# Three dense products tied ahead of the first steps of the band stage and of the latent stage

## The chip, the cores and the metric

The kernel runs on one core of one Trainium2 chip. The metric is the device time of one execution in microseconds (us). The time before is 3204.06 us, the median of three runs (3197.32 to 3205.81).

## The reference, cut to what matters

Two layers of a hybrid streaming encoder are run over 1152 tokens: 1024 of one prompt and 8 x 16 of running streams, model width 1024. Each layer makes one combined input projection, three kinds of attention out of its columns, an output projection and an MLP:

```python
z = h @ w_in                    # h = rmsnorm(x); columns of all three head groups
q_lat, ckv, kr, gq, gk, gv, g_lr, g_out, cq, ck, cv = split(z)
o_mla = latent attention        # q = rmsnorm(q_lat) @ w_qup, keys and values out of ckv, block-causal, 6 heads
o_gla = gated linear attention  # recurrence over chunks of 64, 4 heads
o_ca  = band attention          # each chunk of 64 sees itself and the 8 chunks before, 6 heads
x = x + concat(o_mla, o_gla, o_ca) @ w_out
x = x + relu(rmsnorm(x) @ w_up)**2 @ w_down
```

## The kernel before

Everything is kept with features on the 128 partitions and tokens on the free axis, in three groups of 384 tokens (`G`). A float32 matrix is split into a high and a low part (`wsplit` for weights: one DMA on SP's queue, a rounding copy on ScalarE at L143, a subtraction on VectorE or GpSimd at L131), and a product is the sum of three matmuls per 128 rows. One **dense product** of the input projection is a 128 x 384 tile with 8 x 3 = 24 matmuls; one of the output projection over five of its eight row blocks has 5 x 3 = 15. In the trace these are the groups `z<-hH,win11h`, `z<-oH,wo1h` and the like, all of line L56, the line of the helper `mm`. `win11`, `win14`, `win17`, `win12` are columns of `w_in` in the order in which they are used, `wo1` rows of `w_out`.

A layer goes through these stages: norm and the first three columns of the input projection; the **band stage** (`ca_stage`, 66 to 385 us in layer 0 and 1648 to 1967 in layer 1 of the profiled execution); the gated stage (`gla_stream`, to about 520 and 2104); the **latent stage** (`mla_stream`, 545 to 755 and 2130 to 2340); the rest of the output projection; the MLP. In the first three of these a generator of attention steps, the primary, and a generator of dense products, the filler, are run against each other by `drive`: it keeps account of what either has cost (`pd`, `fd`) and emits a dense product when the filler's share lags behind the primary's. The filler is the rest of the input projection, and then, as heads become ready, the output projection of the gated and band heads.

`drive` only sets the order in which instructions are emitted and their priority (primary steps have the higher one). The order on each engine's queue is then set when the program is built, by a scheduler with a time line of its own, which may emit a dense product ahead of a primary step that it expects to wait. Dependencies of the kind `NOSYNC` bind this scheduler alone: they put one instruction behind another in the queue and leave no wait in the program. Such dependencies already tie each filler matmul to the one `thr` places before it (`fq`).

The steps that the texts below name:

- Band stage. `ca_setup` and `ca_head` load the queries and keys of one head back from DRAM (`cf<-zs_dram`, twelve DMAs on SP's queue), ScalarE rounds them (`qH`, `kS`, L148), GpSimd subtracts (L131). `ca_setup2` loads the values (`cvf`) and transposes them (`cvt`), three groups, one step each. Then come units of 256 queries: scores (`s`, on two banks of PSUM), the maximum (L420), the exponential (L425), scaling (L429), transposes of the probabilities (`ptp`, `PT`), and the product with the values (`pv`).
- Latent stage. `mla_values` makes the values of the first keys (`mv`, `mvhl`), `mla_head` the queries (`q`, out of the weights `wqr`, split into `wqh` and `wql`) and keys (`k`) of a head, group by group; then scores, `ptp` and `pv` as above.
- The dense products of both stages, and `q`, `k` and `mv` of the latent stage, share two banks of PSUM with the tag `d`. A dense product is taken out of its bank by ScalarE in the band stage (`z<-z`, L148) and by VectorE in the latent stage (`xo<-z,xo`).

Of the kernel before, what the change touches and what calls it, by code (L numbers as in the profile page):

```python
# [40 lines left out]
def body(ctx, tc, t):  # L41
# [7 lines left out]
    NOSYNC = mybir.DependencyInfo(mybir.DependencyClass.NoSync, mybir.DependencyReason.SCHED_ONLY)  # L49

    def nm(s):
        uid[0] += 1
        return f"{s}_{uid[0]}"

    def mm(*a, **k):
        i = T.matmul(*a, **k).ins  # L56
        if infill[0]:
            while len(fq) > thr[0]:
                fq.pop(0)
            if len(fq) >= thr[0]:  # L60
                tc.add_manual_dep(i, fq.pop(0), NOSYNC, reason="order")
            fq.append(i.name)

    infill, fq = [False], []

    SQ_POOL = ((5, 7), (2, 5, 7))
    thr = [20]
# [11 lines left out]
    def open_pool(stack, s, side="left"):  # L79
        return stack.enter_context(tc.tile_pool(name=nm(s), bufs=1, reuse_waits="tile", side=side))  # L80
# [19 lines left out]
    def banks(**bufs):  # L100

        pstack.close()
        pcur.clear()
        pcur.update(pool=pstack.enter_context(tc.tile_pool(name=nm("psum"), bufs=1, space=bass.MemoryType.PSUM,
                                                           reuse_waits="tile")), **bufs)
# [116 lines left out]
    def mm_step(outs, w, r, first, last_):  # L222

        for i, (wi, ri) in enumerate(((0, 0), (0, 1), (1, 0))):
            for g, o in outs:
                mm(o, w[wi], r[g][ri], start=first and i == 0, stop=last_ and i == 2)

    STEP = 3 * 3 * 163
# [27 lines left out]
    for l in range(DEPTH):  # L256
# [47 lines left out]
        def behind_norm(ws, put):  # L304

            for g in range(NG):
                for i, w in enumerate(ws):
# [6 lines left out]
        order = (C_CQ + 1, C_CK + 1, C_CV + 1, C_CQ + 2, C_CK + 2, C_CV + 2, C_MIX, C_GQ, C_GK, C_GV, C_GO,  # L314
                 C_GQ + 1, C_GK + 1, C_GV + 1, C_GO + 1, C_CKV)
# [51 lines left out]
            while any(c not in emitted for c in cis):  # L367
                next(filler[0])

        def drive(primary, pc, fc):  # L370

            pd = fd = 0.0
            while True:
                if filler[0] is not None and fd / fc < pd / pc:
                    try:
                        infill[0] = True
                        c = next(filler[0])
                        infill[0] = False
                        if c is not None:
                            fd += c  # L380
                            continue
                    except StopIteration:
                        infill[0] = False
                        filler[0] = None
                try:
                    with tc.high_priority(offset=50):
                        pd += next(primary)
                except StopIteration:
                    break

        def drain():
            if filler[0] is not None:
                for _ in filler[0]:
                    pass
            filler[0] = None
# [224 lines left out]
        def ca_stream(box):  # L620
            with ExitStack() as stack:
                ap = open_pool(stack, "ca")

                def sample():
                    while 2 not in scored:
                        yield 0
                    yield from ca_sample(ap, box)

                c = ca_setup(0, ap)
                ca_head(c, 0, ap)  # L630
                yield 10
                yield from ca_setup2(c, ap, box)
                scored = set()
                for p in range(3):
                    nxt = []

                    def units():
                        for h in range(2):
                            for I in range(4):
                                if I == 2 and h == 0:  # L640
                                    ca_head(c, 1, ap)
                                if I == 1 and h == 1:
                                    ca_scores(c, box)
                                    scored.add(c.p)
                                if I == 2 and h == 1 and p < 2:
                                    nxt.append(ca_setup(p + 1, ap))
                                    ca_head(nxt[0], 0, ap)
                                yield CaUnit(c, h, I)

                    if p < 2:  # L650
                        yield from attention(units(), ap, 5 * P, 2, 3)
                    else:
                        yield from merge(attention(units(), ap, 5 * P, 2, 3), sample())
                    if p < 2:
                        c = nxt[0]
                        yield from ca_setup2(c, ap, box)
# [290 lines left out]
        mla = {}  # L947
# [19 lines left out]
        def mla_keys(mp):  # L967

            ks = [[mp.tile([P, NP_], F32R, name=nm("k")) for _ in range(2)] for _ in range(2)]
            for g in range(NG):  # L970
                lo, hi = g * G, min(NP_, (g + 1) * G)
                kr = piece("krf")
                load(kr[64:96], zs[C_MIX, 64:96, gsl(g)])
                for kH, kL in ks:
                    copy(kH[64:96, lo:hi], kr[64:96, 0:hi - lo])
                    sub_l(V, kL[64:96, lo:hi], kr[64:96, 0:hi - lo], kH[64:96, lo:hi])
            mla["ks"] = ks
# [51 lines left out]
        def mla_values(c, mp, x):  # L1029
            c.v.append(mp.tile([P, 4, 4, 64], F32R, tag="v", name=nm("mvhl"), bufs=3))  # L1030
            if True:
                o = bank("d", "mv")
                for j in range(4):
                    tt = 4 * x + j
                    mm(o[:, j * P:(j + 1) * P], mla["ckv"][tt // 3][:, tt % 3 * P:(tt % 3 + 1) * P],
                       mla["wv"][:, c.p * P:(c.p + 1) * P], start=True, stop=True)
                v_split(c.v[x], o.rearrange("p (n k) -> p n k", k=P))
                yield 4 * 213

        def run(gen):  # L1040
            for _ in gen:
                pass

        def mla_stream(mp):
            mla_keys(mp)
            pairs = []
            for p in range(3):
                c = CaPair()
                c.p, c.q, c.k, c.v = p, {}, {}, []
                pairs.append(c)  # L1050

            extra = []

            def units():
                for p in range(3):
                    c = pairs[p]
                    for h in range(2):
                        for I in range(4):
                            u = MlaUnit(c, h, I)
                            if I == 1 and h == 0:  # L1060
                                run(mla_values(c, mp, 1))
                            if I == 1 and (p, h) != (2, 1):
                                nh = 2 * p + h + 1
                                if nh % 2 == 0:
                                    extra.append(mla_values(pairs[nh // 2], mp, 0))
                                extra.append(mla_head(pairs[nh // 2], nh))
                            if I == 0:
                                while extra:
                                    run(extra.pop(0))
                            yield u  # L1070

            yield from mla_values(pairs[0], mp, 0)
            yield from mla_head(pairs[0], 0)
            for cost in attention(units(), mp, 8 * P, 4, 3):
                yield cost
                if extra:
                    try:
                        yield next(extra[0])
                    except StopIteration:
                        extra.pop(0)  # L1080
# [124 lines left out]
        def ca_stage():  # L1205
            with ExitStack() as outer:
                op = open_pool(outer, "cao")
                cqbd[0] = op.tile([P, N_STREAM, 32], F32, name=nm("cqbd"))
                GP.memset(cqbd[0].rearrange("p s k -> p (s k)"), 0.0)
                box = dict(scs=op.tile([96, N_STREAM, 144], F32, name=nm("scs")),  # L1210
                           vs=op.tile([P, 3, P], F32, name=nm("cvs")))
                yield from ca_stream(box)

        filler = [all_filler()]
        banks(d=2, s=2, tp=2, pv=2)
        thr[0] = TH[0]
        drive(ca_stage(), 100e3, 15 * 8 * STEP)
        banks(d=2, lv=2, tp=2, pv=2)
        weng[0] = V
        thr[0] = TH[1]  # L1220
# [2 lines left out]
        banks(d=2, s=3, tp=2, pv=1)  # L1223
        with ExitStack() as stack:
            thr[0] = TH[2]
            drive(mla_stream(open_pool(stack, "mla")), 165e3, 5 * 8 * STEP)
        drain()


# [451 lines left out]
```

## Time and profile before

| | |
|---|---|
| time, median of three runs | 3204.06 us |
| time of the profiled execution | 3200.47 us |
| its span, first to last instruction | 3198.7 us |
| mean granted TensorE clock | 0.970 |
| TensorE matmul busy (PE) | 3004.8 us, 94% of the span |
| VectorE (DVE) | 2242.8 us, 70% |
| ScalarE (ACT) | 1512.1 us, 47% |
| GpSimd (POOL) | 943.8 us, 30% |
| DMA | 475.58 MB, mean 149 GB/s |

The profile gives busy times of each engine. A row of the time line reads: start, duration, engine, line, operation, output tile and input tiles, shape, count; in brackets the idle time of that engine just before it and what ended it. `PEld` is the loading of weights into TensorE, `SPq` the queue that issues nearly all DMAs. `PEclk` is the clock that was granted to TensorE, as a share of the full one.

### The profile page before, as it was taken

The numbers are of one execution on the slowest core, as the hardware profiler recorded it, in microseconds if no ns is written. First come the engines' busy times: TensorE is split into PE (matmuls) and PEld (weight loads), VectorE is DVE, ScalarE is ACT, GpSimd is POOL, SyncE is SP. The second block draws the span as 40 slices with busy tenths as digits, with TensorE's granted clock in tenths as the row PEclk, the third lists the DMA queues.
The fourth block names the chain that finished last, engine by engine and source line by source line (L and its number), as shares of the span: only waits on it lengthen the run. The fifth ranks groups of instructions, "written<-read, shape, count | busy, mean of one in ns | idle before, by whom it ended". The sixth has DMA issues, their size and how long they took to land.

```text
span 3198.7 us, 51270 instructions
## 1 busy us (share of the span) xinstructions
PE 3004.8 (94%) x17788; PEld 2861.9 (89%) x17788; DVE 2242.8 (70%) x4191; ACT 1512.1 (47%) x3211; POOL 943.8 (30%) x1110
## 2 busy tenths in 40 slices
PE   7999998988999997999999999998989999899998
PEld 7888887877999997999989898878879999889998
DVE  4665597885778775787456655978856877768865
ACT  4554454774534443334245444557754434433342
POOL 4332356553212111111042324555522211111202
PEclk9999999999999998999999999999999999999999
DMA  5333215225445557765443322142353644686553
GB/s 175 106 112 103 94 50 162 67 87 156 136 160 187 171 175 255 254 235 195 134 131 118 100 88 93 54 151 82 93 173 107 208 168 155 221 272 227 175 184 132
DMA packets 297907, 475.58 MB, mean 149 GB/s; under 512 B 35600, under 2 KB 257136, under 8 KB 297648
## 3 DMA queue, kind: packets, MB, share of 16 engines
q1 hardware_dynamic: 297648, 472.31, 45.4%
q8 instruction: 140, 2.29, 0.3%
q14 instruction: 119, 0.97, 0.1%
HBM read 324.32 MB, written 147.85 MB: 148 GB/s over the span
## 4 chain that ended last, share of the span: by engine, by line
PE 67%; DVE 13%; DMA 8%; ACT 5%; issue 3%; SPq 2%; POOL 1%; DVEq 0%; ACTq 0%; POOLq 0%
PE z L56 54%; PE pv L56 3%; PE s L56 2%; PE ptp L71 2%; SPq L74 1%; DMA wr<-in_w_up_dram 1%; ACT P L425 1%; DMA cf<-zs_dram 1%; DMA wr<-in_w_down_dram 1%; PE glao L56 1%; PE lev L56 1%; DMA tL<-td_dram 1%; DMA tH<-td_dram 1%; DVE ga L778 1%; DVE mq L769 1%
## 5 line engine op out<-in xcount | busy, mean ns | idle before, releaser
L56 PE MATMUL z<-hH,wup 128*128 128x384 f32 x1728 | 453.2, 337 | 3.6 <-DVE u L1336 2.9
L56 PE MATMUL z<-uH,wdn 128*128 128x384 f32 x1536 | 411.1, 340 | 13.3 <-ACT uH L148 13.3
L56 PEld LDWEIGHTS z<-hH,wup 128*128 128x128 f32 x1728 | 316.2, 190 | 4.9 <-DVE u L1336 3.6
L56 PEld LDWEIGHTS z<-uH,wdn 128*128 128x128 f32 x1536 | 283.3, 191 | 15.3 <-ACT uH L148 15.2
L56 PE MATMUL z<-hL,wup 128*128 128x384 f32 x864 | 291.2, 337 | 0.0
L1355 POOL TENSOR_TENSOR ws<-wr 128x512 f32<-128x512 f32 x60 | 84.2, 1404 | 667.0 <-DMA wr<-in_w_down_dram 260.4
L56 PE MATMUL z<-uL,wdn 128*128 128x384 f32 x768 | 260.8, 340 | 0.5 <-DVE uL L131 0.3
L56 PE MATMUL z<-tH,wds 128*128 128x384 f32 x768 | 210.8, 343 | 7.6 <-DMA tH<-td_dram 7.6
L1324 ACT ACTIVATE wdn<-wr 128x1024 fp32r<-128x1024 f32 x96 | 101.7, 1060 | 236.7 <-PE z L56 210.0
L425 ACT ACTIVATE P<-s,ng 128x320 f32<-128x320 f32 (+5 forms) x288 | 157.5, 551 | 98.5 <-DVE ng L422 60.2
L1337 ACT ACTIVATE u<-u 128x384 f32<-128x384 f32 x192 | 99.5, 519 | 214.2 <-DVE u L1336 199.7
L148 ACT ACTIVATE PT<-ptp 128x512 fp32r<-128x512 f32 (+3 forms) x288 | 128.5, 460 | 116.9 <-PE ptp L71 115.6
L56 PE MATMUL z<-ts,wus 128*128 128x384 f32 x1008 | 181.4, 336 | 1.3 <-ACT wus L1324 1.0
L131 DVE TENSOR_TENSOR PT<-ptp,PT 128x512 fp32r<-128x512 f32 (+3 forms) x288 | 146.4, 516 | 48.3 <-ACT PT L148 40.4
L1474 DVE TENSOR_TENSOR x<-z,x 128x384 f32<-128x384 f32 x176 | 96.2, 551 | 118.2 <-PE z L56 117.9
L56 PEld LDWEIGHTS z<-ts,wus 128*128 128x128 f32 x1008 | 174.8, 188 | 3.2 <-ACT wus L1324 2.3
L56 PEld LDWEIGHTS z<-hL,wup 128*128 128x128 f32 x864 | 163.7, 189 | 0.0
L71 PE MATMUL ptp<-ident,P 128*128 128x128 f32 x792 | 139.8, 282 | 18.4 <-DVE PT L131 7.9
L56 PEld LDWEIGHTS z<-tH,wds 128*128 128x128 f32 x768 | 141.7, 191 | 11.0 <-DMA tH<-td_dram 10.7
L420 DVE TENSOR_REDUCE ng<-s 128x1 f32<-128x320 f32 (+5 forms) x288 | 146.5, 515 | 5.9 <-PE s L56 2.7
L56 PEld LDWEIGHTS z<-uL,wdn 128*128 128x128 f32 x768 | 146.6, 191 | 2.3 <-DVE uL L131 2.1
L131 DVE TENSOR_TENSOR wdn<-wr,wdn 128x1024 fp32r<-128x1024 f32 x96 | 119.5, 1245 | 28.7 <-ACT wdn L1324 27.7
(466 smaller groups left out, 8580.0 us busy)
## 6 DMA issues: line engine op xcount, KB each, us to landing
wr<-in_w_down_dram SPq DMA_DIRECT2D x128, 512.0 KB, 3.7
td_dram<-td SPq DMA_DIRECT2D x256, 192.0 KB, 2.1
wr<-in_w_up_dram SPq DMA_DIRECT2D x72, 512.0 KB, 4.0
u_dram<-u SPq DMA_DIRECT2D x164, 192.0 KB, 2.4
ur<-u_dram SPq DMA_DIRECT2D x160, 192.0 KB, 4.4
tH<-td_dram SPq DMA_DIRECT2D x128, 192.0 KB, 4.1
tL<-td_dram SPq DMA_DIRECT2D x128, 192.0 KB, 4.2
zs_dram<-z SPq DMA_DIRECT2D x102, 192.0 KB, 1.9
```

The lines of the kernel that those rows point to most:

```text
L56: i = T.matmul(*a, **k).ins
L71: T.transpose(out, in_, idn)
L74: nc.sync.dma_start(dst, src)
L131: eng.tensor_tensor(lo, src, h.bitcast(F32), ALU.subtract)
L148: S.activation(o, i, AF.Copy, scale=scale)
L420: V.tensor_reduce(ng[:, x:x + 1], sc[x][:, :hi - lo], AX.X, ALU.max, negate=True)
L425: S.activation(pr[:, lo:hi], sc[x][:, :hi - lo], AF.Exp, bias=ng[:, 0:1], accum_out=ss[:, x:x + 1])
L769: (GP if h else V).tensor_tensor(q2[hr, h, :w // 2].rearrange("p (n s) -> p n s", s=s), mv[hr, :, 1, :], qv[hr, :, 1, :], ALU.mult)
L1324: S.activation(h, raw, AF.Copy)
L1337: S.activation(u, u, AF.Square)
L1355: GP.tensor_tensor(s1, a21, a22, ALU.add)
L1474: V.tensor_tensor(x, o, x if xo is None else xo, ALU.add)
```

## The change

`drive` gets a number `lead`. In each of its first `lead` rounds it takes one dense product from the filler before anything else, keeps the name of that product's last matmul in `tie`, and the next matmul that is emitted through `mm` outside the filler is put behind it by a `NOSYNC` dependency. The band stage and the latent stage of both layers are driven with `lead` = 3; the gated stage is not. The products taken are counted into `fd`, so that the accounting holds back the next ones until the primary has caught up.

```diff
@@ mm
             fq.append(i.name)
+        elif tie[0] is not None:
+            tc.add_manual_dep(i, tie[0], NOSYNC, reason="order")
+            tie[0] = None
+        last_mm[0] = i.name
 
     infill, fq = [False], []
+
+    tie, last_mm = [None], [None]
...
-        def drive(primary, pc, fc):
+        def drive(primary, pc, fc, lead=0):
 
             pd = fd = 0.0
             while True:
+                if lead > 0 and filler[0] is not None:
+                    lead -= 1
+                    infill[0] = True
+                    fd += next(filler[0]) or 0
+                    infill[0] = False
+                    tie[0] = last_mm[0]
                 if filler[0] is not None and fd / fc < pd / pc:
...
-        drive(ca_stage(), 100e3, 15 * 8 * STEP)
+        drive(ca_stage(), 100e3, 15 * 8 * STEP, 3)
...
-            drive(mla_stream(open_pool(stack, "mla")), 165e3, 5 * 8 * STEP)
+            drive(mla_stream(open_pool(stack, "mla")), 165e3, 5 * 8 * STEP, 3)
```

No instruction is added to or taken from the program; the order changes, on every engine, in two places of each layer: the first half of the band stage (up to about 252 us in layer 0, 1844 in layer 1) and most of the latent stage. Outside these the order is the same but for a few rows at the end of the gated stage and in the MLP. In the band stage the first two primary steps issue no matmul through `mm` (loads, and transposes, which go past it), so that the tie that remains is that of the third product: the first scores stand behind it. In the latent stage each of three steps has its own.

**First place: TensorE's queue in the band stage of layer 0, at the transposes of the values and the third to fifth scores.** In the names, `cvt` are the transposed values, `s` scores, `z` dense products, `ptp` transposed probabilities. Before:

```order
L71 MATMUL cvt_783<-ident,cvf_781 128x128 x2
L56 MATMUL s_833<-kS_704,qH_702 128x512
L56 MATMUL s_833<-kS_704,qL_703 128x512
L71 MATMUL cvt_783<-ident,cvf_781 128x128
L71 MATMUL cvt_793<-ident,cvf_791 128x128 x3
L56 MATMUL s_887<-kS_704,qH_702 128x320
L56 MATMUL s_887<-kS_704,qL_703 128x320
L56 MATMUL s_888<-kS_704,qH_702 128x320
L56 MATMUL s_888<-kS_704,qL_703 128x320
L71 MATMUL ptp_848<-ident,P_807 128x128
L71 MATMUL ptp_934<-ident,P_818 128x128 x2
L56 MATMUL z_1084<-hH_192,win14h_1080 128x384
```

And now, from the first transposes of the values on:

```order
L77 MATMUL cvt_803<-ident,cvf_801 128x128 x3
L56 MATMUL z_1084<-hH_234,win14l_1081 128x384
L56 MATMUL z_1166<-hH_282,win14h_1080 128x384
L56 MATMUL z_1166<-hL_283,win14h_1080 128x384
L56 MATMUL z_1166<-hH_282,win14l_1081 128x384
L56 MATMUL s_878<-kS_738,qH_736 128x384
L56 MATMUL s_878<-kS_738,qL_737 128x384
L56 MATMUL s_889<-kS_738,qH_736 128x512
L56 MATMUL s_889<-kS_738,qL_737 128x512
L77 MATMUL cvt_839<-ident,cvf_837 128x128 x3
L56 MATMUL z_1166<-hH_288,win14h_1080 128x384
```

Before, no dense product stood between the first transposes of the values and the second transposes of probabilities; now the third dense product stands ahead of the first scores, and the fourth and fifth (`z_1084`, `z_1166`, of the weights `win14`) run through this place.

**Second place: the same queue some rows on, at the second product with the values (`pv_1050`).** Before:

```order
L56 MATMUL pv_1050<-PT_967,cvhl_771 128x256 x4
L56 MATMUL s_977<-kS_704,qH_702 128x320
L56 MATMUL s_977<-kS_704,qL_703 128x320
L56 MATMUL pv_1050<-PT_968,cvhl_771 128x256
L71 MATMUL ptp_1071<-ident,P_900 128x128
L56 MATMUL s_978<-kS_704,qH_702 128x320
L56 MATMUL s_978<-kS_704,qL_703 128x320
```

And now:

```order
L56 MATMUL s_967<-kS_738,qH_736 128x320
L56 MATMUL s_967<-kS_738,qL_737 128x320
L56 MATMUL s_968<-kS_738,qH_736 128x320
L56 MATMUL s_968<-kS_738,qL_737 128x320
L56 MATMUL pv_1050<-PT_995,cvhl_799 128x256 x4
L77 MATMUL ptp_1071<-ident,P_956 128x128 x4
L56 MATMUL pv_1050<-PT_996,cvhl_799 128x256 x4
L77 MATMUL ptp_1112<-ident,P_956 128x128
L56 MATMUL pv_1149<-PT_1063,cvhl_799 128x256
L56 MATMUL z_1261<-hH_372,win14h_1080 128x384
```

Before, 45 matmuls of dense products stood between the fifth scores (`s_887`, `s_888`) and `pv_1050`; now, between the fifth scores (here `s_943`, `s_944`) and `z_1261`, there are 31 matmuls of attention and none of a dense product.

**Third place: SP's queue at the start of the latent stage of layer 0.** `wqr` are the weights of the queries, `wo1r` those of the dense products, `xpart_dram<-xo` stores the results of earlier dense products. Before:

```order
L77 DMA xpart_dram<-xo_5934 128x384
L138 DMA wqr_6127<-in_w_qup_dram 128x768
L77 DMA xpart_dram<-xo_5960 128x384
L77 DMA xpart_dram<-xo_6044 128x384
L138 DMA wo1r_6282<-in_w_out_dram 128x640
L138 DMA wo1r_6441<-in_w_out_dram 128x640
```

And now:

```order
L83 DMA xpart_dram<-xo_5934 128x384
L144 DMA wo1r_6127<-in_w_out_dram 128x640
L80 DMA wkT_6165<-in_w_kT_dram 64x128
L83 DMA xpart_dram<-xo_5960 128x384
L83 DMA xpart_dram<-xo_6044 128x384
L144 DMA wqr_6153<-in_w_qup_dram 128x768
L144 DMA wo1r_6183<-in_w_out_dram 128x640
```

The load of the queries' weights has gone behind two stores, and the weights of the second dense product stand where it was. On TensorE's queue there, a first dense product of 15 matmuls (`z<-oH,wo1h`) now stands ahead of `mv`, where it stood behind it; a second stands ahead of the first group of `q`, and a third between its first and second groups. Before, the second stood behind the first seven score tiles (at 568 us) and the third behind the thirteenth (at 587 us).

## The prediction

> **What bounds the kernel now.** I read the first rows of the page, then the chain of waits by engine, then busy times in stretches cut at the two stages that the change touches:
>
> ```profile
> span 3198.7 us, 51270 instructions
> PE 3004.8 (94%) x17788; PEld 2861.9 (89%) x17788; DVE 2242.8 (70%) x4191; ACT 1512.1 (47%) x3211; POOL 943.8 (30%) x1110
> PE 67%; DVE 13%; DMA 8%; ACT 5%; issue 3%; SPq 2%; POOL 1%; DVEq 0%; ACTq 0%; POOLq 0%
> 45.28 19.63 PE z L56 x113
> 100.00:385.00 285.00, 272.88 (x1741) 256.51 (x1740) 166.41 (x404) 131.16 (x344) 82.58 (x141) 0.99 0.33 105
> ```
>
> TensorE is the bound: busy for 94% of the span, and two thirds of the chain. So no dense product can be hidden; it can only stand where TensorE would otherwise wait. The fourth row, from the chain, prices it: 113 matmuls in 19.63 us are 0.174 each, so 24 take 4.2 us and 15 take 2.6. The last row (time, PE, PEld, DVE, ACT, POOL busy, clock, DMA share, GB/s) shows that most of the band stage has little to win. The change acts where the two stages start.
>
> **The start of the band stage.** Stretches of equal meaning in both layers, and inside them the pieces in which the granted clock falls to one half:
>
> ```profile
> 66.00:100.00 34.00, 29.49 (x149) 27.40 (x148) 16.56 (x45) 15.20 (x42) 14.69 (x19) 0.85 0.58 176
> 1648.00:1683.00 35.00, 28.59 (x149) 26.58 (x148) 17.76 (x45) 15.39 (x42) 15.03 (x21) 0.85 0.57 174
> 72.30:75.70 3.40, 1.36 (x9) 1.04 (x8) 0.00 (x0) 2.47 (x5) 2.40 (x3) 1.00 0.53 155
> 75.70:79.10 3.40, 3.40 (x13) 3.40 (x12) 2.63 (x8) 1.67 (x6) 2.80 (x5) 0.50 0.96 304
> 82.50:86.00 3.50, 1.82 (x10) 0.94 (x8) 3.38 (x9) 3.17 (x10) 3.13 (x2) 0.99 0.55 162
> 86.00:92.80 6.80, 6.02 (x18) 5.19 (x19) 5.08 (x15) 4.12 (x14) 5.23 (x8) 0.50 0.53 168
> 1662.90:1666.30 3.40, 0.61 (x4) 0.20 (x2) 3.08 (x2) 1.29 (x4) 2.61 (x2) 1.00 0.65 191
> ```
>
> TensorE is idle for 34.00 - 29.49 = 4.5 us in layer 0 and 6.4 in layer 1, and a mean clock of 0.85 takes 15% of the rest of the time away, 5.1 and 5.2 us. The cause is seen inside: a stretch of 3.4 us with 1.36, 1.82 or 0.61 us of work is followed by one at 0.50. Both losses together are 9.6 and 11.7 us. What the idle time waits for:
>
> ```profile
> 75.26 0.51 PE L56 MATMUL s<-kS,qH 128*128 128x256 f32 x2 [2.04 <-POOL kS L131]
> 84.15 0.52 PE L71 MATMUL cvt<-ident,cvf 128*128 128x128 f32 x3 [0.92 <-PE cvt L71]
> 85.30 0.41 PE L56 MATMUL s<-kS,qH 128*128 128x320 f32 x1 [0.62 <-ACT P L425]
> 91.13 0.99 DVE L429 TENSOR_SCALAR P<-P,ss 128x640 f32<-128x640 f32 x1
> 1657.12 0.51 PE L56 MATMUL s<-kS,qH 128*128 128x256 f32 x2 [1.61 <-POOL kS L131]
> 1667.43 0.88 PE L71 MATMUL cvt<-ident,cvf 128*128 128x128 f32 x3 [3.92 <-DVE cvhl L131]
> ```
>
> The first scores wait for keys that came back from DRAM (2.04, 1.61 us), the transposes for the emptying of their banks (0.92, 3.92). What the change does here, step by step:
>
> 1. The third product stands ahead of the first scores. It needs 4.2 us, and the keys come within 2; so 2.04 and 1.61 us of idle time are filled, and the 3.4 us of half clock that follow in layer 0 go with them. The scores start some 2 us later; the fourth product stands behind them in the queue.
> 2. The fourth and fifth products run through the transposes, where 0.92, 0.62 and 3.92 us were idle. The copies that free their two banks stand on ScalarE behind roundings of `cf`, which wait for DMAs; I cost that at nothing, since the products ahead of them cover 4.2 us each, and at up to 1.5 us if SP's extra stores ahead of `cf` push those roundings back.
> 3. The bill comes in the second place shown above: 31 matmuls of attention with no dense product among them. A step's chain, from fifth scores to scaled probabilities, takes 92.12 - 85.30 = 6.8 us. The 31 rows take some 3.1 us at 0.1 us each (estimate: small matmuls are 128 or 256 columns wide, a dense one of 384 takes 0.174). So about 3.7 us idle are new, say 4, and they lie close enough for a stretch at half clock as in the rows above: 3.4 to 6.8 us of it, each costing half, 1.7 to 3.4 us; I take 2.5. That leaves 6.5 us lost per layer. Bounds: nothing lost, or the chain wholly bare with the old half clock on top, 6.8 + 5.1 = 11.9.
>
> By both layers: (9.6 - 6.5) + (11.7 - 6.5) = 8.3 us gained; between 21.3 gained and 2.5 lost. Further on, up to 252 us, the products are in step again at the fifth `pv`, so nothing is counted.
>
> One rule speaks on the clock. The Trainium skill, "TensorE: Matmul & The Clock Gate", Part 1, says the clock halves after a whole idle window of about 3.4 us; this trace disagrees, since 2.04 us of idle time within 3.4 us were followed by 0.50. By that rule the gaps would have cost only themselves, and this stage would give 4.5 + 6.4 - 8 = 2.9 us instead of 8.3.
>
> **The start of the latent stage.** Here the rows are TensorE's own, then those of the weights of the queries:
>
> ```profile
> 549.00:560.20 11.20, 8.08 (x45) 6.60 (x43) 6.41 (x11) 5.35 (x11) 6.59 (x6) 1.00 0.51 162
> 560.20:575.00 14.80, 14.26 (x87) 13.10 (x88) 12.15 (x37) 11.13 (x31) 6.59 (x7) 1.00 0.08 28
> 575.00:586.70 11.70, 9.10 (x48) 7.40 (x47) 10.23 (x24) 9.56 (x26) 6.35 (x6) 0.85 0.16 50
> 586.70:598.40 11.70, 11.70 (x83) 11.54 (x82) 9.12 (x28) 8.18 (x23) 4.23 (x8) 1.00 0.27 78
> 546.54 0.33 SPq L138 DMA_DIRECT2D wqr<-in_w_qup_dram  x1
> 546.97 4.33 SPq L77 DMA_DIRECT2D xpart_dram<-xo  x2
> 550.45 0.85 ACT L143 ACTIVATE wqh<-wqr 128x768 fp32r<-128x768 f32 x1 [2.41 <-DMA wqr<-in_w_qup_dram]
> 551.38 1.85 POOL L131 TENSOR_TENSOR wql<-wqr,wqh 128x768 fp32r<-128x768 f32 x1 [1.63 <-ACT wqh L143]
> 553.28 0.19 PEld L56 LDWEIGHTS q<-qlH,wql 128*128 128x128 f32 x1 [0.42 <-POOL wql L131]
> 557.02 0.41 PE L56 MATMUL q<-qlH,wqh 128*128 128x384 f32 x1 [1.74 <-DVE rq L997]
> ```
>
> 4. SP's queue: the load of `wqr` goes behind the two stores, which end at 546.97 + 4.33 = 551.3 because the second waits for its result. From issue (546.54) to the end of `wql` (553.23) it took 6.7 us; so `wql` now ends at about 558, and the third matmul of `q`, which waited for it at 553.28, comes 4.8 us later. On ScalarE `mvhl` stands behind `wqh` and is late too, but it only holds the bank that the same `q` needs.
> 5. The product ahead of `q` (2.6 us) covers part of this; 2.2 us stay bare. The product between the first and second groups of `q` takes the place of the 1.74 us that the third group waited for its bank, but the keys now wait for the second group's bank as the third had waited: I take 1.2 us, between nothing and 1.74. First scores: 4.8 + 2.6 - 1.74 + 1.2 = 6.9 us later, of which 5.2 are moved work. Cost: 1.7 us.
> 6. From 560.2 to 598.4 these two products are gone. Where TensorE was full (14.26 of 14.80, and 11.70 of 11.70) that gives time back, unless VectorE takes over as the bound: 12.15 us busy in 14.80, and 0.56 less without the result of one product. I take three quarters of 5.2 back, 3.9, and 1.3 lost; the bounds are all and nothing.
> 7. Nobody else waits: from the fourth `pv` on the products are in step with the old order, and the later wave of the stage changes place without changing count.
>
> So 3.0 us lost per layer, 6.0 in both, if layer 1, with the same order and 8.46 us busy in its first 11.50, behaves alike:
>
> ```profile
> 2132.50:2144.00 11.50, 8.46 (x48) 7.02 (x46) 6.75 (x11) 5.26 (x10) 6.91 (x6) 1.00 0.56 168
> ```
>
> Bounds per layer: 3.1 us gained (all idle time of 549 to 560.2 filled, `wqr` in time), or 1.7 + 5.2 lost, and 1.7 more for one stretch at half clock; both layers: 6 gained to 17 lost.
>
> **The sum.** -8.3 + 6.0 = -2.3 us against the profiled execution's 3200.47, so 3198.2. The median of the runs shown lies 3.6 us above that execution, so on its scale 3201.8, say 3202. A measurement of this kernel can tell about 0.3%, 9.6 us, from no change.
>
> **The rivals.**
>
> - *Faster: the gaps go and nothing comes back.* For it: the fourth and fifth products reach as far as the fifth scores, and ScalarE, at 15.20 us busy in 34, has room to run the chain faster than 6.8 us. Against it: the queue order, which has no dense product to fill the waits of the second place. With 17 of the 21.3 us won and the latent stage as I have it with 2 lost, 3204 - 15 = 3189.
> - *Slower: steps left without cover cost their whole chain.* For it: products spent early are missing later, in both stages; VectorE is at 12.15 of 14.80 right where the latent stage loses them. Against it: in 575 to 586.7, without a product, TensorE still worked 9.10 of 11.70. The band stage would then end at its loss of 2.5 us, the latent stages at 5 each: 3204 + 12.5 = 3216. It decides from 6 us of bare chain per start on.
> - *No effect: TensorE waits as long as before, elsewhere.* The order changes, as shown, so this can only be by balance. Each start would give and take the same; 3204.
>
> **How the numbers follow.** My forecast has 0.42, no effect 0.13, both within 0.3%: same 0.55. The faster rival has 0.24, the slower 0.21: I put the gain first by a little, since the idle time and the half clock of the band stage are measured and the bill is an estimate. The bounds run from 3204 - 21 - 6 to 3204 + 2.5 + 17; the range for 8 in 10 cuts about a tenth on each side: 3188 to 3215. The likeliest case alone spans 3195 to 3209.
>
> **What would show it.** In the new profile: the first scores of the band stage with no wait for keys behind a third product, and a clock of 1.00 at 75 to 80 us (step 1); transposes of the values without 0.92 and 3.92 us of waiting (2); waits of 3 to 5 us between the fifth scores and the sixth product, with half clock behind them (3); `wqh` waiting for `wqr` until about 555, the third matmul of `q` at 558 less what the band stage has won (4); the first scores of the latent stage about 7 us later against its start (5); VectorE near 90% behind them (6). I am wrong if the second place shows no waits (then faster), or if the latent stage starts late by more than 10 us or the band stage's `cf` roundings hold the banks of the fourth and fifth products (then slower).

## The result, and the profile after

The changed kernel takes 3226.38 us (median of five, 3222.02 to 3234.32) beside 3205.81 us of the kernel before (3197.32 to 3210.09): ratio 1.0066, 95% interval 1.0048 to 1.0084. The forecast was 3202, within 3188 to 3215. It is slower by 20.6 us where 2.3 us of gain were expected.

The head of the page of after:

```profile
span 3220.2 us, 51259 instructions
PE 3012.2 (94%) x17788; PEld 2858.6 (89%) x17788; DVE 2245.4 (70%) x4191; ACT 1511.8 (47%) x3211; POOL 946.3 (29%) x1110
```

Stretches of it (start and end, length, then busy time and count of PE, PEld, DVE, ACT, POOL, the granted clock, DMA share, GB/s):

```profile
64.70:85.00 20.30, 20.26 (x120) 19.78 (x119) 7.91 (x16) 7.44 (x18) 10.01 (x11) 1.00 0.76 227
85.00:100.00 15.00, 11.49 (x67) 9.49 (x66) 11.26 (x33) 9.47 (x28) 5.15 (x11) 1.00 0.39 110
100.00:252.00 152.00, 140.86 (x847) 131.34 (x847) 99.77 (x252) 72.84 (x200) 44.69 (x75) 0.97 0.34 105
293.20:357.70 64.50, 64.34 (x420) 59.12 (x419) 26.06 (x68) 22.76 (x59) 10.54 (x29) 0.89 0.26 82
```

and the stretches of before that answer to the last two:

```profile
100.00:252.00 152.00, 145.09 (x899) 136.66 (x897) 96.67 (x255) 75.73 (x206) 45.89 (x78) 0.99 0.35 110
289.30:348.00 58.70, 58.55 (x419) 54.37 (x418) 26.02 (x68) 22.70 (x59) 10.53 (x29) 1.00 0.28 88
```

The start of the band stage is as full as hoped for: 20.26 of 20.30 us, at full clock. Behind it, from 100 to 252 us, TensorE is busy for 4.2 us less and the clock is lower. And in a place that the prediction does not speak of, 293 to 358 us, the same work takes 5.8 us more with next to no idle time by the records (0.16 us of 64.50): only the clock differs, 0.89 against 1.00.

To say where the time went, the ends of the same dense products are compared in both traces (counted in each layer, 24 matmuls to a product, 15 in the output projection; at these cuts attention has also got equally far):

| between the ends of dense products | layer 0, before → after | layer 1 |
|---|---|---|
| band stage up to the running streams (8th to 40th; 9th to 40th) | 228.5 → 233.8 us | 225.8 → 227.9 us |
| the running streams' product with the values (40th to 48th) | 58.6 → 64.3 | 58.6 → 64.3 |
| latent stage with the end of the gated one (from the 68th; the 65th) | 230.4 → 232.4 | 259.0 → 263.0 |

These add up to 24.9 us; everything else gives 3.4 back, since the two executions differ by 21.5. The expectations below number the products otherwise: their 62nd and 78th are the 32nd and 40th here. Executions differ in where the half clock strikes, so the experiments are also compared by the means of these rows over several traces.

### The profile page after: what moved, and what is told of

Read it like the earlier page. It is cut to its first block, busy times and chain, and to the rows that moved or that the text cites. A ratio compares the mean times of both kernels' runs of the same rounds, so it can differ in the third digit from the quotient of the medians.

```text
span 3220.2 us, 51259 instructions
## 1 busy us (share of the span) xinstructions
PE 3012.2 (94%) x17788; PEld 2858.6 (89%) x17788; DVE 2245.4 (70%) x4191; ACT 1511.8 (47%) x3211; POOL 946.3 (29%) x1110
```

## The experiments

The order on TensorE in the running streams (`caso`, 16-column matmuls of `vc` with `ptc`, two records each) is the same before and after, so the half clock there called for a reason first. **Theory A**: the granted clock changes on a grid of 3.41 us (in each trace all stretches at half clock begin on one such grid and, but for one cut off by the end of the execution, last one to six times 3.41 us; in before and after one to four times), and the place of this work on the grid decides. **Theory B**: the lead brings it.

**One stage at a time.** The last argument of one of the two `drive` calls is left out.

```diff
-            drive(mla_stream(open_pool(stack, "mla")), 165e3, 5 * 8 * STEP, 3)
+            drive(mla_stream(open_pool(stack, "mla")), 165e3, 5 * 8 * STEP, 0)
```

> Lead 3 in the band stage alone, none in the latent stage. In the changed kernel's trace the band stage is won 7.0 and 8.1 us at its start, loses 12.2 and 10.1 us behind it (up to the 62nd dense product), and loses 5.8 and 5.7 us more in 293 to 358 and 1884 to 1948 us, where TensorE is full in both kernels and only the granted clock differs (0.89 against 1.00). Theory A, the half clock there is where the work happens to fall on a grid of 3.4 us, not a consequence of the lead: start and bill as above, 7.3 lost over both layers, and the 11.5 us come or go: 3206 + 7 to 3206 + 19 us; the trace shows which. Theory B, the lead itself brings it: 3225 us, with 13.65 us at half clock in both layers.

Measured: 3212.14 us, ratio 1.0017 (1.0001 to 1.0034), with 13.65 us at half clock in the running streams of both layers of its trace. That is 0.9 us under the lowest time expected, although this trace has all of the half clock that was to make 3225: either other executions have less of it, or the lead costs less than the first trace said.

```diff
-        drive(ca_stage(), 100e3, 15 * 8 * STEP, 3)
+        drive(ca_stage(), 100e3, 15 * 8 * STEP, 0)
```

> Lead 3 in the latent stage alone; the band stage of layer 0 has the order of before. In the changed kernel's trace the latent stages are 2.0 and 4.0 us longer than before. Both theories: 3206 + 6 = 3212 us. Theory A allows 13.65 us at half clock in the stretch of the running streams (near 320 and 1910 us) here too, though the order there is that of before, and then up to 11.5 us more; theory B has none there.

Measured: 3215.58 us, 1.0038 (1.0021 to 1.0055), no half clock in the running streams. Each stage costs something by itself; on the half clock this does not decide.

**The ties, and one product instead of three.**

```diff
-                    tie[0] = last_mm[0]
```

> Lead 3 in both stages as in the change, but no dependency ties a step behind its product. In layer 0's band stage the order on TensorE is that of the changed kernel row for row; in the latent stage few rows differ. If the lead alone does it, the time is that of the changed kernel within 0.3%: 3217 to 3230 us, the spread from the half clock. If the ties do it, it comes back to 3206 us.

Measured: 3219.42 us, 1.0041 (1.0025 to 1.0056). The lead alone makes most of it; its interval overlaps that of the change.

```diff
-        drive(ca_stage(), 100e3, 15 * 8 * STEP, 3)
+        drive(ca_stage(), 100e3, 15 * 8 * STEP, 1)
...
-            drive(mla_stream(open_pool(stack, "mla")), 165e3, 5 * 8 * STEP, 3)
+            drive(mla_stream(open_pool(stack, "mla")), 165e3, 5 * 8 * STEP, 1)
```

> One dense product ahead instead of three, in both stages, tied. The bill of the band stage should go with the products spent early: one product of 4.2 us ahead of the first scores covers about as much waiting as was there (2.04 us), and the second place of the prediction has its products back. Theory of spent products: band stage 0 to 4 us won per layer, latent stage within 2 us: 3198 to 3210 us, and 11.5 us more if the half clock of the running streams comes. If it is the first product alone that delays everything: as slow as the change, 3220 to 3226 us.

Measured: 3212.79 us, 1.0026 (1.0010 to 1.0043). With one product the start still has a wait of 3.00 us at the transposes of the values, with 10.24 us of half clock begun at it, and the running streams pay in both layers of the trace:

```profile
84.36 0.90 PE L77 MATMUL cvt<-ident,cvf 128*128 128x128 f32 x3 [3.00 <-DVE cvhl L137]
```

So no gain. The time lies above 3198 to 3210 and inside what was expected if the half clock came on top.

**The place on the grid.** More work per layer, as repeats of the first matmul of a dense product, some 25 us ahead of the running streams: 16 in the kernel before, 6 in the changed one.

```diff
+                    if ci == 8 and g == 0:
+                        for _ in range(16):
+                            T.matmul(o, w[0][:, 0, :], hs[0][g][0], start=True, stop=True)
                     dense(o, w, lambda k: hs[k][g], KD)
```

> The kernel before, with 16 more matmuls (the first of a dense product, repeated) in front of one dense product of each layer, about 25 us ahead of the running streams: 2.8 us of work per layer, and everything behind it falls 2.8 us later on the grid. No lead. In the four layers traced so far without a lead in the band stage the 78th dense product ended 1.83 to 1.93 us behind an edge of that grid, with no half clock in the running streams; in the eight with one 1.05 to 1.68 us, with 13.65 us of it each time. Theory A (the place on the grid decides): the end moves to about 1.3 us behind an edge, half clock for 13.65 us in both layers, 3206 + 5.6 + 11.5 = 3223 us. Theory B (the lead decides): none, 3206 + 5.6 = 3211 us.

Measured: 3214.31 us, 1.0031 (1.0015 to 1.0047). In layer 1 there are 10.24 us at half clock in the running streams, with no lead; in layer 0 none, and its place there is not the one reckoned (other half clocks ahead may have moved it). So the expected 3223 us was wrong, theory B too.

> The changed kernel with 6 such matmuls more per layer, 1.04 us. Theory A: the place moves to 2.1 to 2.7 us behind an edge, past the 1.83 from which no half clock was seen, so that both layers lose it and the kernel gets faster by more work: 11.5 less and 2.1 more, 3219 to 3226 becomes 3210 to 3217 us. Theory B: half clock in both layers as before, 3221 to 3228 us.

Measured: 3217.07 us, 1.0035 (1.0019 to 1.0051): the changed kernel has six matmuls more per layer and no half clock there in either layer. Rows of after in the running streams, from the time line, and two stretches there:

```profile
318.97 1.13 PE L56 MATMUL caso<-ptc,vc 128*64 128x16 f32 x18
320.07 0.85 PE L56 MATMUL caso<-ptc,vc 128*64 128x16 f32 x12
```

```profile
319.30:322.70 3.40, 3.40 (x43) 2.70 (x41) 1.36 (x5) 1.04 (x5) 0.00 (x0) 0.99 0.07 20
322.70:336.30 13.60, 13.60 (x60) 11.25 (x61) 3.38 (x10) 2.87 (x8) 0.41 (x2) 0.50 0.04 15
```

And of the run with six more, whose first such row begins at 321.45 us:

```profile
312.00:350.00 38.00, 38.00 (x283) 34.95 (x283) 15.43 (x40) 13.91 (x38) 6.42 (x17) 1.00 0.28 86
```

TensorE is busy by the records for 3.40 of 3.40 us, mostly with records of 16-column matmuls, 0.06 us each, between scores, and 0.50 follows for 13.6 us. In all 24 layers traced with this order of the running streams (twelve runs) the time from the last edge of the grid to the first of these 18 records separates them without an exception: 0.25 to 1.15 us, no half clock (9 layers); 1.86 to 3.41 and 0 to 0.10 us, 10.24 or 13.65 us of it (15 layers).

**The weights of the queries earlier.** In the kernel with the lead in the latent stage alone:

```diff
-            if hd % 3 == 0:
+            if hd == 3:
                 mla["wq"] = wsplit(t["w_qup"][l, hd // 3], [2, 3, P], "wq", GP)
...
         with ExitStack() as stack:
+            mla["wq"] = wsplit(t["w_qup"][l, 0], [2, 3, P], "wq", GP)
```

> Lead 3 in the latent stage alone, but the load of the queries' first weights stands ahead of the three products, as early as before. TensorE's order in the latent stage is that of the run with lead 3 in the latent stage alone. That run's latent stages have 4.6 and 4.3 us more idle time than before. Theory: the late weights make it (step 4 of the prediction), then the idle time goes back to before's and the time to 3206 to 3209 us. Rival: the products missing behind the start make it (step 6), then 3213 to 3216 us as without this edit.

Measured: 3220.36 us, 1.0048 (1.0029 to 1.0067), so no help; it lies above both ranges. What the queries no longer wait for, the dense product ahead of them does (its weights `wo1r` are now behind `wqr`; TensorE, then ScalarE):

```profile
561.47 0.69 PE L56 MATMUL z<-oH,wo1h 128*128 128x384 f32 x1 [3.14 <-ACT wo1h L149]
560.68 0.74 ACT L149 ACTIVATE wo1h<-wo1r 128x640 fp32r<-128x640 f32 x1 [3.21 <-DMA wo1r<-in_w_out_dram]
```

The order of its band stage is that of before, and its running streams pay 10.24 and 13.65 us: with the run above, theory B is out.

**The small matmuls together.** A yield behind each of them lets the scheduler put the 36 of the second and third head pair (32 of 16 columns, 4 of 128) in one row between dense products:

```diff
                         mm(po[hr, 16 * s:16 * s + 16], vc[:, s, hr], pc[:, s, hd * 16:hd * 16 + 16],
                            start=(s == 0), stop=False)
+                        yield 120
                     mm(po[hr, :P], cbox["vs"][:, hp, hr], pn[:, :, hd * 16:hd * 16 + 16], start=False, stop=True)
-                    yield 1100
+                    yield 140
```

With the lead in the band stage alone:

> Lead 3 in the band stage alone, and the running streams' product emitted in smaller steps (a yield behind each of its matmuls), by which their 16-column matmuls stand together, 36 in a row between two dense products, instead of spread over 9 us among scores and transposes. If the half clock there comes from some 7 us of small matmuls in a row, whose share of the grid's stretches depends on their place, a cluster of some 2 us between dense products stays under the limit wherever it falls: no half clock, 3212 - 11.5 = 3201 us, faster than before. If not: 3212 us.

Measured: 3200.93 us, 0.9989 (0.9973 to 1.0005). The stretch up to the 48th product, and the cluster:

```profile
291.80:350.10 58.30, 56.42 (x420) 53.22 (x419) 25.83 (x67) 22.06 (x58) 10.61 (x29) 1.00 0.29 94
339.50:343.10 3.60, 3.60 (x72) 3.56 (x72) 0.00 (x0) 0.28 (x1) 0.00 (x0) 1.00 0.00 0
```

58.3 us instead of 64.4, and the clock stays at 1.00 though the cluster's 72 records fill a whole length of the grid. What keeps the clock up there is not shown; that they take 3.6 us instead of being spread over 9 with scores and transposes is what the edit changed. With no lead, twice:

> No lead, and the 16-column matmuls of the running streams together as in the kernel with lead 3 in the band stage. Of the six layers traced without a lead four had no half clock there and two had (10.2 and 13.65 us): so before pays it in some executions. Theory A (place on the grid): the edit takes 5.8 us off each layer in the executions that paid, 2 to 6 us of the median, and the lead's own cost in the band stage, 3.5 + 2.2 us by the mean of the traces, is not there: 3194 to 3200 us, faster than with the lead. Rival, that the lead in the band stage gains where the half clock is away: then this is slower than the 3201 us of the run with both.

> The kernel before with the 16-column matmuls together once more, for a second trace: no half clock in the running streams in either layer, 3190 to 3202 us.

Measured: 3198.23 us, 0.9976 (0.9963 to 0.9990), and 3191.86 us in one run. With the whole change, and the change again beside it:

> The change with the 16-column matmuls together. Theory A: the half clock of the running streams is gone and the two bills stay, 3204 + 5.7 + 8.6 less what before pays of it itself (2 to 6 us): 3212 to 3217 us, 8 to 11 us under the change of this call. If half clock there is no part of the loss: as the change.

> The changed kernel once more, for its time beside the same runs of before and for a second trace. By the means of the stages so far it pays 5.7 us in the band stages, 8.6 in the latent stages and, where the running streams fall so, 11.5 us of half clock: 3218 to 3228 us. If the first time was high by chance, 3216 to 3220 as without the ties.

Measured: 3212.42 us, 1.0032 (1.0018 to 1.0046), beside 3224.15 us, 1.0067 (1.0050 to 1.0083). All 16 layers traced with the matmuls together (eight runs) have no half clock in this stretch; three have 3.41 us of it some 6 us behind its end. It was 11.7 us of the change's time, and 4.7 us of before's: the trace of before pays in neither layer, so it would be other executions of it that pay.

**The bill of the band stage.** First, whether it comes from counting the three products:

```diff
-                    fd += next(filler[0]) or 0
+                    next(filler[0])
```

> Lead 3 in the band stage alone, not counted in the filler's account, so that the next dense products aren't held back. Theory that the bill (12.2 and 10.1 us up to the 62nd dense product) comes from holding them back: the 7 to 8 us won at the start stay, the bill falls to the moved work, and up to the 78th product the stage is 1 to 5 us shorter than before; three products fewer are left for its end, which has 58 us of full TensorE. 3198 to 3206 us, and 11.5 more if the running streams pay. Rival, that the bill comes from the other heads' setup falling at other times: as with the count, 3212 us.

Measured: 3206.59 us, 1.0011 (0.9998 to 1.0024), one of two layers paying in the running streams. In this one trace it took 229.6 us up to the 40th product and in layer 1 227.7, not less than before: leaving out the count does not win the 1 to 5 us expected. Then one instruction. After, VectorE and GpSimd at the second head pair, and what TensorE waits for:

```profile
217.45 2.54 DVE L435 TENSOR_TENSOR ng<-ng 128x1 f32<-128x1 f32 x1
217.39 0.28 POOL L596 COPY cqbd<-cf 64x128 f32<-64x128 f32 x1
217.64 2.33 POOL L137 TENSOR_TENSOR win6l<-win6r,win6h 128x1024 fp32r<-128x1024 f32 x1
220.70 0.63 PE L56 MATMUL s<-kS,qH 128*128 128x320 f32 x1 [2.76 <-ACT P L438]
```

```profile
216.90:220.30 3.40, 0.78 (x5) 0.60 (x5) 3.37 (x4) 1.62 (x6) 3.32 (x4) 0.99 0.27 77
220.30:227.10 6.80, 6.17 (x19) 5.77 (x20) 6.34 (x14) 2.40 (x8) 3.00 (x6) 0.50 0.39 117
```

A minimum of two columns takes 2.54 us, begins inside a copy of GpSimd's and ends with GpSimd's subtraction of weights (219.99 and 219.97); exponential, transposes and scores wait behind it, and 6.8 us at half clock follow. The Trainium skill, "SBUF — State Buffer", "SBUF: two separate sides", says that VectorE and GpSimd share a pair of ports: whichever of a GpSimd instruction and a VectorE operation with two inputs from SBUF starts first has the pair for its whole instruction, and the other waits. The trace agrees: the minimum waits out the copy and the subtraction behind it. Before, the same minimum stood two places further back, behind two multiplications by `rope`, and took less than half as long:

```profile
217.69 2.35 POOL L131 TENSOR_TENSOR win6l<-win6r,win6h 128x1024 fp32r<-128x1024 f32 x1
219.03 1.02 DVE L422 TENSOR_TENSOR ng<-ng 128x1 f32<-128x1 f32 x1
```

So the minimum is taken with one input:

```diff
-                    V.tensor_tensor(ng[:, 0:1], ng[:, 0:1], ng[:, 1:2], ALU.min)
+                    V.tensor_reduce(ng[:, 0:1], ng[:, 0:2], AX.X, ALU.min)
```

> The changed kernel, but the minimum of the two half maxima of a score tile (VectorE, 128x1, two inputs from SBUF) is taken by a reduction over the pair, with one input. TensorE's order in layer 0's band stage is unchanged. Theory, the blocked instruction: at 217 us that 128x1 operation takes 2.54 us and ends with GpSimd's subtraction of weights (2.33 us, begun 0.2 us later); scores wait 2.76 us for the exponential behind it and a second half-clock stretch of 3.41 us follows; with one input it isn't held: about 0.2 us, the wait under 1 us, the half clock behind it 3.41 us or none instead of 6.83. That is 3 to 4 us per layer: 3224 becomes 3215 to 3219 us. Rival, that GpSimd holds VectorE whatever its inputs are, or that the scores would wait for something else next: as the change, 3221 to 3226 us.

Measured: 3206.65 us, 1.0001 (0.9986 to 1.0016), far more than expected. Groups of this instruction (count, busy, mean ns) in before, after and here, then rows of the time line here:

```profile
L422 DVE TENSOR_TENSOR ng<-ng 128x1 f32<-128x1 f32 x96 | 30.7, 320 | 1.5
```

```profile
L435 DVE TENSOR_TENSOR ng<-ng 128x1 f32<-128x1 f32 x96 | 38.4, 400 | 1.6
```

```profile
L435 DVE TENSOR_REDUCE ng<-ng 128x1 f32<-128x2 f32 x96 | 14.3, 149 | 1.6
```

```profile
215.94 0.15 DVE L435 TENSOR_REDUCE ng<-ng 128x1 f32<-128x2 f32 x1
217.70 0.64 PE L56 MATMUL s<-kS,qH 128*128 128x320 f32 x1 [1.26 <-ACT P L438]
```

```profile
217.50:220.90 3.40, 3.20 (x10) 3.06 (x11) 3.13 (x8) 2.19 (x8) 3.20 (x6) 0.50 0.43 128
```

The mean of 96 falls from 400 to 149 ns, the wait from 2.76 to 1.26 us, the half clock behind it from 6.83 to 3.41. At this place the reduction runs just ahead of the subtraction (216.02 us), so these rows alone do not show that it would not be held; all 96 do: 38 of them begin while a GpSimd operation on two tensors runs, and none takes more than 0.16 us, where the longest minimum of after takes 2.56. Part of this run's gain is luck of the grid: one layer of its trace has no half clock in the running streams. Both edits together, with the lead in the band stage alone (the same kernel twice), with none, and with the whole change:

> Lead 3 in the band stage, the 16-column matmuls together, and the minimum by a reduction. If the lead's loss in the band stage (2.9 and 2.4 us by the mean of the traces up to the 78th product) is mostly the blocked instruction, this run wins 3 to 8 us on the run without the reduction (3201 us): 3193 to 3198 us, and the lead in the band stage costs nothing or gains. If not: 3199 to 3203 us.

> Lead 3 in the band stage with both edits, once more: the best so far, ratio 0.9955, for the comparison with the whole change and a second time: 0.994 to 0.997.

> No lead, the 16-column matmuls together, the minimum by a reduction: the same two edits for the kernel before. Where no lead stands, the same operation took 1.02 us at this place; 0 to 2 us per layer are to be had, in the latent stage the order changes: 3192 to 3199 us. Against the run with the lead beside it this tells what the lead in the band stage is worth without either trap.

> The whole change with both edits: 16-column matmuls together, minimum by a reduction. If the two traps were all that the band stage lost and the latent stage pays its own bill (5.2 and 1.7 us by the mean of the traces, 6.9 in both layers), this stands 5 to 10 us above the run with the lead in the band stage alone and the same edits: ratio to before 0.9965 to 0.999. Rival, the latent bill too was an effect of blocked instructions: as that run, 0.9955.

Measured, in this order: 3194.94 us, 0.9955 (0.9938 to 0.9972); 3196.93 us, 0.9985 (0.9972 to 0.9998); 3198.04 us, 0.9976 (0.9960 to 0.9993); 3203.96 us, 1.0002 (0.9989 to 1.0014). The ratios of the second and the last lie above the expected ones. The first two are one kernel, and their intervals only just touch: the median of before moved between 3202.9 and 3208.8 us from one set of runs to the next, so that 0.3% between sets is not told. Over two such sets, the whole change is no faster with both edits (1.0002) than with the reduction alone (1.0001). Beside each other, the whole change stands 7.0 us above the lead in the band stage alone, as expected (5 to 10). Beside each other, too, the lead in the band stage with both edits stands 3.1 us below none (3194.94 and 3198.04), but their intervals overlap. Without the lead the reduction brings nothing (0.9976 with it and without).

The means over the traces, to the 40th product (16 and 6 extra matmuls taken off): no lead, 229.1 us in layer 0 and 224.0 in layer 1 (seven traces, single ones 227.1 to 231.8 and 222.3 to 225.8); lead of three, 232.6 and 226.6 (seven; 231.6 to 236.2 and 224.5 to 228.6); lead and reduction, 229.0 and 223.9 (four; 225.6 to 233.2 and 222.4 to 225.4). The stage can be cut once more at the 30th product, just ahead of the held minimum (215.0 us in before), where attention has got equally far too. Up to this cut the means are 154.1 and 150.2 us with no lead, 154.5 and 149.7 with the lead, 155.2 and 150.2 with lead and reduction. From it to the 40th they are 74.9 and 73.7; 78.1 and 76.9; 73.8 and 73.7. So what the start wins is spent before the cut with or without the reduction, and the 3.2 us per layer that the lead loses lie behind it, where the reduction saves them.

In the latent stage: no lead, 230.4 and 259.8 us (ten traces); lead of three, 235.5 and 261.8 (eight, without that of the earlier weights), 7.1 us in both layers together.

## Why the prediction was wrong, step by step

**Steps 1 and 2 (the start of the band stage) held.** After, first scores, the three transposes of the values, and the waits of the "second place":

```profile
76.11 0.50 PE L56 MATMUL s<-kS,qH 128*128 128x256 f32 x2
80.68 0.49 PE L77 MATMUL cvt<-ident,cvf 128*128 128x128 f32 x3
82.53 0.49 PE L77 MATMUL cvt<-ident,cvf 128*128 128x128 f32 x3
85.47 0.49 PE L77 MATMUL cvt<-ident,cvf 128*128 128x128 f32 x3
88.81 0.44 PE L77 MATMUL ptp<-ident,P 128*128 128x128 f32 x2 [0.90 <-ACT cvs L154]
89.72 0.51 PE L56 MATMUL pv<-PT,cvhl 128*128 128x256 f32 x2 [0.47 <-ACT PT L154]
91.72 0.41 PE L56 MATMUL s<-kS,qH 128*128 128x320 f32 x1 [0.49 <-ACT P L438]
93.26 0.74 PE L56 MATMUL pv<-PT,cvhl 128*128 128x256 f32 x4 [0.47 <-ACT PT L154]
94.98 0.74 PE L56 MATMUL pv<-PT,cvhl 128*128 128x256 f32 x4 [0.33 <-DVE PT L137]
96.77 0.44 PE L56 MATMUL z<-hH,win14h 128*128 128x384 f32 x1 [0.82 <-ACT z L154]
```

No wait for keys, none at the transposes, no half clock at 75.7 or 86.0.

**Step 3 failed, and in its last sentence.** The second place cost what was said: the waits above are 3.48 us where "say 4" stood, and without the half clock of 2.5. But "further on, up to 252 us, the products are in step again at the fifth `pv`, so nothing is counted" was wrong. At the transposes of the second pair's values there are waits of 1.35, 1.44 and 0.54 us with a stretch at 0.50 behind them, and at 217 us the held minimum:

```profile
171.60 0.55 PE L77 MATMUL cvt<-ident,cvf 128*128 128x128 f32 x3 [1.35 <-DVE cvhl L137]
173.59 0.30 PE L77 MATMUL ptp<-ident,P 128*128 128x128 f32 x1 [1.44 <-DVE cvhl L137]
174.43 0.77 PE L77 MATMUL ptp<-ident,P 128*128 128x128 f32 x5 [0.54 <-ACT cvs L154]
```

```profile
175.90:179.30 3.40, 3.40 (x12) 3.40 (x12) 2.97 (x10) 1.79 (x6) 2.01 (x5) 0.50 0.83 247
```

Equal counts of products and `pv` say nothing about the order on the other engines: the minimum had moved two places on VectorE. In before no such wait stands at the transposes:

```profile
172.32 0.49 PE L71 MATMUL cvt<-ident,cvf 128*128 128x128 f32 x3
173.70 0.27 PE L71 MATMUL ptp<-ident,P 128*128 128x128 f32 x1
```

By the means the term is 6.1 us lost (3.5 + 2.6) instead of 8.3 gained. By the same means the reduction takes all of it away (229.0 and 223.9 against 229.1 and 224.0), and then the lead is worth next to nothing in this stage (the pair of runs beside each other leaves room for 3 us): what is won at the start is waited for later, as the rival "no effect" had it for the whole. That the held instruction is the trap rests on the edit, its groups and the cut at the 30th product; that the waits at the second pair's values take the gain of the start was read from one trace and not tried.

**A term was missing.** The half clock of the running streams lies outside the rows on which the order differs, so no cost was looked for there. It is the largest: 11.7 us of the change, where before pays 4.7 of its own, so 7.0 of the difference.

**Steps 4 to 7 (latent stage) held in size, not in every part.** Here the late weights, from SP's queue to the first scores:

```profile
562.68 0.40 SPq L144 DMA_DIRECT2D wqr<-in_w_qup_dram  x1
565.90 0.85 ACT L149 ACTIVATE wqh<-wqr 128x768 fp32r<-128x768 f32 x1 [3.42 <-DMA wqr<-in_w_qup_dram]
566.83 1.82 POOL L137 TENSOR_TENSOR wql<-wqr,wqh 128x768 fp32r<-128x768 f32 x1 [2.72 <-PE z L56]
568.70 0.19 PEld L56 LDWEIGHTS q<-qlH,wql 128*128 128x128 f32 x1 [0.39 <-POOL wql L137]
575.76 0.44 PE L56 MATMUL q<-qlH,wqh 128*128 128x384 f32 x1 [1.69 <-DVE xo L1180]
578.70 0.68 PE L56 MATMUL s<-k,qH 96*128 96x256 f32 x3 [1.10 <-ACT k L154]
```

The stage begins 10.5 us later than before; `wql` was forecast to end at 558 (568.5 with the 10.5) and ends at 568.65, the third matmul of `q` starts at 568.70. The first scores come 18.5 - 10.5 = 8.0 us later (560.22 before) against 6.9. The third group of `q` still waits 1.69 us for its bank, which step 5 had filled by a product; the keys, which step 5 had wait 1.2, do not. Up to the first `pv` 1.7 us came back, where step 6 took 3.9 for its stretch; more came back later in the stage. The sum, 7.1 by the means and 7.0 by the last pair of runs, stands against 6.0. What costs it is open: with the weights early (step 4) the wait moved to the dense product ahead and nothing was won.

**The slower rival** (3216) named steps that lose their cover, from 6 us per start on; there was some of that, but what carried the result past it, a held VectorE instruction and a clock that falls with TensorE full, is not in it. The account: 6.1 us in the band stages, 7.0 in the latent ones, 11.7 - 4.7 in the running streams, 20.1 of the 20.6 measured. That it comes so close is luck: each term is known to some 4 us, and the same terms would put the lead in the band stage alone at 6.1 + 7.0 = 13.1 above before, where it measured 6.5.

## What to carry to other kernels

When dense work is spent earlier, the later waits do not vanish with it; compare the order of every engine, not TensorE's alone, up to where all of them agree, and look there for short two-input VectorE operations that come to stand beside long GpSimd ones. Keep matmuls of few columns together between dense ones rather than spread among scores and transposes. A kernel whose time hangs on where its thin stretches fall on the clock's grid wins or loses some 0.2% per layer by unrelated edits, so judge an edit by traces of several executions.

## What was not expected of the hardware

- TensorE busy by the records for 3.40 of 3.40 us was followed by a granted clock of 0.50 for 13.65 us. The Trainium skill, "TensorE: Matmul & The Clock Gate", Part 1, knows the half clock after an idle window; here it also follows windows that the records show full, of 16-column matmuls among scores and transposes. What is counted there no run shows: streamed columns instead of recorded busy time would fit these windows, but not the cluster of 72 records, which has no half clock directly behind it in 16 layers.
- Six more matmuls per layer (1.04 us) took 13.65 us at half clock away in each layer of the changed kernel.
- A VectorE minimum over 128x1 took 2.54 us beside a GpSimd instruction of 2.33 us, in layer 1 at the same place 2.56 us; as a reduction with one input, 96 of them averaged 0.149 us.
